# Query and key projected by channel, rotary on whole tiles, score operands stacked by SBUF-to-SBUF transfers, and the two tap chains interleaved

## The chip, the cores and the metric

The kernel runs on one core of one Trainium2 chip. The metric is device time in microseconds of one execution. Three runs of the kernel before gave a median of 925.05 us (922.57 to 925.73).

## The reference

Two layers of a decoder trunk over 512 tokens of width 1024, in float32. Each layer normalises the residual, projects it into nine blocks of 256 columns, feeds four token mixers with them, and projects the four outputs back onto the residual. Then come a routed mixture of 16 experts and a gated per-layer input. The change touches the differential attention and, in a detail, the 31-tap convolution:

```python
u = n @ w_in[i]                       # 1024 -> 9 x 256
a_val, a_gate, pool_in, q, k, v, gb, gc, sv = split(u)
# conformer: glu = a_val * sigmoid(a_gate); y = causal depthwise conv, 31 taps; layernorm; silu
# differential attention: 4 heads, 2 components each, 32 channels per component
rot = concat([-x[..., 16:], x[..., :16]])          # apply_rope, on q and on k
x   = x * cos + rot * sin
sc  = einsum("bqhcd,bkhcd->bhcqk", qb, k) * 32 ** -0.5
a   = softmax(where(mask, sc, -inf))
a   = a[:, :, 0] - lam * a[:, :, 1]
o   = einsum("bhqk,bkhe->bqhe", a, v)              # rmsnorm follows, then the output projection
```

## The kernel before

Every float32 operand of a large product is split into a high part that the matrix engine takes exactly and a low part that holds the rest. A product is then three matmuls: high by high, low by high, high by low (`mm3`). ScalarE makes the high part (a cast), VectorE the low part (a subtraction). This holds for weights too: `w.get` hands out one half of a weight load of 1 MB, split by a ScalarE cast (`wh`) and a VectorE subtraction (`wl`).

`project` forms the nine blocks. Most are projected by channel in `cm_unit`: the weight is the stationary operand and all 512 tokens stream past it, so that the output tile has channels on the partitions. Query and key are projected by token instead: the normalised tokens `nhi`, `nlo` are stationary and 512 weight columns stream past, into four tiles `o` of 128 tokens by 512 channels. The rotary embedding (`rotate`) works on half a token tile at a time with four VectorE operations on 128x128 or 128x256 elements.

`attend` needs query and key with channels on the partitions. For each of the 16 head components the score product is one matmul over 96 rows: three blocks of 32 rows that hold high, low, high of the query (`QT`) against high, high, low of the key (`KT`). Before the change `stack` and `stack_lo` write the three blocks side by side into the tile `qks` (two ScalarE operations and one VectorE subtraction for each token tile and side), and `qkt` turns them with TensorE transposes, four at a time, which ScalarE copies into `QT` and `KT`.

The order of the instructions is written by hand. The attention loop runs over 18 steps `n`; the list `TICK` gives the order of the parts of a step, and `ROT`, `STK`, `STL` say in which step which piece of rotary and stacking is done. The output projection (`wo_mm`) is the filler for TensorE: `filler(n, k)` issues k halves of six matmuls each, and `FILL1`, `FILL2` hold k for each step. VectorE's filler are the convolution's taps: 31 for each of two channel tiles, each one operation on 128x512 elements that adds to the accumulator `acc`. They wait in a queue from which `tick` takes as many as its budget allows, first all of channel tile 0, then all of tile 1. Weights come by transfers that SyncE issues in program order from one queue; where an instruction of that queue waits, all behind it wait.

Pools of SBUF are opened and closed as a stack on two sides. `KT` stands in the pool `kp`, which is opened where `ntp`, the pool of `nhi` and `nlo`, was closed.

Of the kernel before, what the change touches and what calls it, by code (L numbers as in the profile page):

```python
# [11 lines left out]
F32 = mybir.dt.float32  # L12
F32R = mybir.dt.float32r
# [26 lines left out]
K_ID, K_RC, K_IO, K_VT, K_DE, K_IW, K_MK, K_TRI, K_COS, K_SIN = 0, 128, 160, 288, 304, 320, 322, 450, 578, 834  # L40
NCON, NCON2, NCON3 = 322, 256, 512
# [6 lines left out]
FILL2 = [4, 0, 1, 0, 0, 1, 0, 4, 1, 0, 0, 1, 0, 0, 0, 1, 2, 1, 2, 1, 2, 2, 4, 2, 2, 2, 0, 0, 0]  # L48
# [4 lines left out]
TICK = "qkt max add av out exp f1 stl turn stk due lo rot score hi f2 comb".split()  # L53
TAPS = [1.8, 2.4, 2.4, 4.8, 1.8, 1.2, 5.4, 0, 0, 0.6, 3.6, 0, 0, 1.2, 3.4, 0, 1.0, 3.4]
ROT = {0: [(2, 0)], 2: [(2, 1)], 3: [(3, 1)], 4: [(3, 0)]}
STK = {0: [(1, 1)], 2: [(2, 0)], 3: [(2, 1)], 5: [(3, 0)], 7: [(3, 1)]}
STL = {1: [(1, 1)], 3: [(2, 0)], 5: [(2, 1)], 6: [(3, 0)], 8: [(3, 1)]}
# [110 lines left out]
class _Kernel:  # L168
# [91 lines left out]
    def run(self):  # L260
# [163 lines left out]
    def cm_unit(self, between=None, cost=0.0):  # L424
        o = [self.mm([128, S]) for _ in range(2)]
        for hf in range(2):
            self.cm_half(o, self.w.get(between=between if hf == 0 else None), hf)
            self.ticks.tick(BUDGET - cost if hf == 0 else BUDGET)
        return o

    def project(self):
# [165 lines left out]
        rope = vp.tile([128, 2, NT, 2, 32], F32, name="rope")  # L597
        nc.sync.dma_start(rope, self.A["con"][:, K_COS:K_COS + NCON3].rearrange("p (c t a d) -> p c t a d", c=2, t=NT, a=2))
        qr = self.qr = [vp.tile([128, 16, 32], F32, name=f"qr{i}") for i in range(NT)]
# [5 lines left out]
        def qk(i, half, k0):  # L605
            ts = slice(i * 128, (i + 1) * 128)
            hi, lo = (t.rearrange("p (c n) -> p c n", c=2) for t in half)
            for c in range(2):
                k = k0 + c
                self.mm3(o[i], self.nhi[:, k, ts], self.nlo[:, k, ts], hi[:, c], lo[:, c], k == 0, k == 7)  # L610

        half = w.get(between=ev_v)
        o = [self.mm([128, 512]) for _ in range(NT)]
        for hf in range(2):
            if hf:
                half = w.get()
            for i in range(NT):
                qk(i, half, 2 * hf)
            tk.tick(BUDGET)
        hv = [w.get(1), w.get(1)]  # L620
        for i in range(NT):
            for hf in range(2):
                qk(i, hv[hf], 4 + 2 * hf)
        w.make_hi(w.cur + 2)

        def rotate(i, b):

            bs = slice(8 * b, 8 * b + 8)
            x4 = qr[i][:, bs] if i else o[0].rearrange("p (a d) -> p a d", d=32)[:, bs]
            rt, rs = (vp.tile([128, 8, 32], F32, name=nm) for nm in ("rt", "rs"))  # L630
            cos, sin = rope[:, 0, i, b, None, :], rope[:, 1, i, b, None, :]
            V.tensor_mul(rs[:, :, 0:16], x4[:, :, 16:32], sin[:, :, 0:16].to_broadcast([128, 8, 16]))
            V.tensor_mul(rs[:, :, 16:32], x4[:, :, 0:16], sin[:, :, 16:32].to_broadcast([128, 8, 16]))
            V.tensor_mul(rt, x4, cos.to_broadcast([128, 8, 32]))
            V.tensor_add(qr[i][:, bs], rs, rt)

        self.rotate = rotate
        for b in range(2):
            rotate(0, b)
        for i in range(1, NT):  # L640
            SC.copy(qr[i].rearrange("p a d -> p (a d)"), o[i])
        w.make_lo()
        self.ntp.close_()
        self.banks(3, 1)

# [47 lines left out]
    def attend(self):  # L693
        V, T, SC, w, tk, sm, l = self.V, self.T, self.SC, self.w, self.ticks, self.sm, self.l
        mhi, mlo, h = self.mhi, self.mlo, self.h
        kp = self.pool("kp", side=self.side[0])
        KT = kp.tile([96, 8, S], F32R, name="KT")
        xp = self.xp
        a2 = self.pool("a2", side=self.side[1])
        QT = {}  # L700
        stk = {}


        qks = xp.tile([128, 2, 8, 3, 32], F32, name="qks", bufs=1)

        def stack(i, p):
            s_ = stk[i, p] = qks[:, p]
            SC.copy(s_[:, :, 0, :].bitcast(F32R), self.qr[i][:, 8 * p:8 * p + 8])
            SC.copy(s_[:, :, 2 - p, :], s_[:, :, 0, :])

        def stack_lo(i, p):
            s_ = stk[i, p]
            V.tensor_sub(s_[:, :, 1 + p, :].bitcast(F32R), self.qr[i][:, 8 * p:8 * p + 8], s_[:, :, 0, :])

        def qkt(i, p, b):
            s_ = stk[i, p]
            if p == 0 and b == 0:
                QT[i] = kp.tile([96, 8, 128], F32R, name="QT", bufs=2)
            pt = self.tr([128, 4, 128])
            for c in range(4):  # L720
                T.transpose(pt[:96, c], s_[:, 4 * b + c].rearrange("p a d -> p (a d)"), self.ident)
# [855 lines left out]
```

## Time and profile before

| | |
|---|---|
| median of three runs | 925.05 us |
| the profiled execution's own time | 925.41 us |
| span of its instructions | 923.6 us |
| mean granted TensorE clock | 0.973 of full speed |
| TensorE busy | 858.0 us, 93% |
| VectorE busy | 715.4 us, 77% |
| ScalarE busy | 519.1 us, 56% |

The profile is of one execution. Busy shares are averages over stages with different limits. What the change is worth is read from the stage that it touches, in each of the two layers: the end of the projections and the attention loop (in the first layer from about 99 to 200 us).

### The profile page before, as it was taken

The numbers are of one execution on the slowest core, as the hardware profiler recorded it, in microseconds if no ns is written. First come the engines' busy times: TensorE is split into PE (matmuls) and PEld (weight loads), VectorE is DVE, ScalarE is ACT, GpSimd is POOL, SyncE is SP. The second block draws the span as 40 slices with busy tenths as digits, with TensorE's granted clock in tenths as the row PEclk, the third lists the DMA queues.
The fourth block names the chain that finished last, engine by engine and source line by source line (L and its number), as shares of the span: only waits on it lengthen the run. The fifth ranks groups of instructions, "written<-read, shape, count | busy, mean of one in ns | idle before, by whom it ended". The sixth has DMA issues, their size and how long they took to land. (4 is left out here: it accounts for less than half of the span.)

```text
span 923.6 us, 12348 instructions
## 1 busy us (share of the span) xinstructions
PE 858.0 (93%) x4393; PEld 687.6 (74%) x4393; DVE 715.4 (77%) x1182; ACT 519.1 (56%) x945; POOL 151.2 (16%) x214
## 2 busy tenths in 40 slices
PE   7999988897999999979979999989979999998994
PEld 5888876685677777767878887767847777776783
DVE  4599989966788888746676998998478888885674
ACT  4322246853687878745433233487347778776453
POOL 2040001122222211101010300022131222111101
PEclk9999999998999999999999999989979999999998
DMA  9222230158799979563322223110958998882602
GB/s 354 106 92 96 98 114 1 46 193 309 270 347 363 370 271 340 227 234 146 114 92 92 92 103 112 49 46 24 373 216 307 359 370 324 317 321 91 260 24 91
DMA packets 35775, 179.02 MB, mean 194 GB/s; under 512 B 8064, under 2 KB 8320, under 8 KB 18944
## 3 DMA queue, kind: packets, MB, share of 16 engines
q1 hardware_dynamic: 23472, 148.49, 43.1%
q0 software_dynamic: 9792, 20.99, 6.2%
q10 hardware_dynamic: 2448, 8.73, 2.6%
q8 instruction: 35, 0.57, 0.2%
q14 instruction: 28, 0.23, 0.1%
HBM read 171.89 MB, written 23.07 MB: 211 GB/s over the span
## 5 line engine op out<-in xcount | busy, mean ns | idle before, releaser
L239 DVE TENSOR_TENSOR wl<-wr,wh 128x1024 fp32r<-128x1024 f32 x212 | 253.1, 1220 | 41.4 <-ACT wh L228 40.1
L228 ACT CAST wh<-wr 128x1024 fp32r<-128x1024 f32 x212 | 216.2, 1053 | 91.1 <-PE mm L256 60.9
L255 PE MATMUL mm<-wh,xTh 128*128 128x512 f32 x256 | 113.9, 445 | 1.0 <-ACT xTh L221 1.0
L483 DVE SCALAR_TENSOR_TENSOR acc<-glu,cwh,acc 128x512 f32<-128x512 f32 x120 | 100.5, 837 | 3.4
L257 PE MATMUL mm<-wh,xTl 128*128 128x512 f32 x256 | 101.2, 395 | 1.2 <-DVE xTl L222 1.2
L256 PE MATMUL mm<-wl,xTh 128*128 128x512 f32 x256 | 100.5, 392 | 0.0
L257 PE MATMUL mm<-nhi,wl 128*128 128x512 f32 (+1 forms) x224 | 77.3, 345 | 2.5 <-DVE wl L239 2.5
L255 PE MATMUL mm<-nhi,wh 128*128 128x512 f32 (+1 forms) x224 | 77.1, 344 | 0.0
L256 PE MATMUL mm<-nlo,wh 128*128 128x512 f32 (+1 forms) x224 | 77.0, 344 | 0.0
L255 PEld LDWEIGHTS mm<-wh,xTh 128*128 128x128 f32 x256 | 48.1, 188 | 16.9 <-issue 6.7
L1241 PE MATMUL mm<-wr,hT 128*128 128x512 f32 x128 | 60.2, 592 | 0.0
L1198 POOL DMA_INDIRECT xg<-xnd,ix x32 | 35.4, 1105 | 149.8 <-PE tr L251 136.8
L256 PEld LDWEIGHTS mm<-wl,xTh 128*128 128x128 f32 x256 | 48.2, 188 | 15.3 <-DVE wl L239 6.2
L257 PEld LDWEIGHTS mm<-wh,xTl 128*128 128x128 f32 x256 | 48.0, 188 | 12.9 <-DVE xTl L222 2.9
L255 PE MATMUL mm<-wh,mhi 128*128 128x512 f32 x128 | 54.0, 422 | 1.0 <-DVE h L750 1.0
L1203 POOL DMA_INDIRECT yd<-ys,ix x32 | 32.3, 1010 | 122.9 <-ACT ys L1243 107.3
L255 PE MATMUL mm<-wh,n3h 128*128 128x512 f32 x128 | 50.6, 395 | 0.0
L257 PE MATMUL mm<-wh,mlo 128*128 128x512 f32 x128 | 50.3, 393 | 0.0
L256 PE MATMUL mm<-wl,mhi 128*128 128x512 f32 x128 | 50.0, 391 | 0.0
L257 PE MATMUL mm<-wh,n3l 128*128 128x512 f32 x128 | 49.9, 390 | 0.0
L256 PE MATMUL mm<-wl,n3h 128*128 128x512 f32 x128 | 49.9, 390 | 0.0
L257 PEld LDWEIGHTS mm<-nhi,wl 128*128 128x128 f32 x224 | 42.4, 189 | 8.2 <-DVE wl L239 3.2
(236 smaller groups left out, 1861.6 us busy)
## 6 DMA issues: line engine op xcount, KB each, us to landing
wr<-wgu SPq DMA_DIRECT2D x62, 1024.0 KB, 9.1
wr<-wdn SPq DMA_DIRECT2D x30, 1024.0 KB, 10.8
wr<-win SPq DMA_DIRECT2D x13, 1024.0 KB, 6.2
wr<-wout SPq DMA_DIRECT2D x8, 1024.0 KB, 4.8
wr<-wpg SPq DMA_DIRECT2D x8, 1024.0 KB, 13.8
yt<-yd SPq DMA_DIRECT2D x12, 512.0 KB, 8.1
wr<-wqk SPq DMA_DIRECT2D x4, 1024.0 KB, 4.8
xnd<-xn ACTq DMA_DIRECT2D x8, 512.0 KB, 4.0
```

The costliest lines, as they stand in the source:

```text
L228: self.SC.copy(hi, src)
L239: self.V.tensor_sub(lo, src, h32)
L255: self.T.matmul(o, lh, rh, start=first, stop=False)
L256: self.T.matmul(o, lh, rl, start=False, stop=False)
L257: self.T.matmul(o, ll, rh, start=False, stop=last)
L483: V.scalar_tensor_tensor(acc[:, m], glu[:, m, k:k + S], self.cwh[:, m, k:k + 1], acc[:, m], op0=ALU.mult, op1=ALU.add)
L1198: return self.G.indirect_dma_start(out=dst, out_offset=None, in_=self.xnd[:, :], in_offset=bass.IndirectOffsetOnAxis(ap=col, axis=0), boun ...
L1203: return self.G.indirect_dma_start(out=self.yd[:, :], out_offset=bass.IndirectOffsetOnAxis(ap=col, axis=0), in_=src, in_offset=None, bound ...
L1241: self.T.matmul(o[nh], hT[:, c], wc[:, ns], start=(c == 0), stop=(c == 1))
```

## The change

The columns of query and key in the input weight are put in another order on the host, so that both can be projected with `cm_unit`. The two output tiles of such a unit hold the first and the second half of the 32 channels of all eight head components, 128 rows each. The rotary embedding then takes three VectorE operations on 128x512 elements for each of the two tiles, one ScalarE cast and one VectorE operation for the low part. The query's scale is applied in that cast. The rows of `QT` and `KT` are filled by transfers from SBUF to SBUF: each moves 128 rows of 512 floats, 256 KB, into 16 rows. There are six for the key and six for the query in a layer, all in SyncE's queue. `QT` now holds all 512 queries.

```diff
-            for u in (1, 0, 2, 7, 8, 6, 5):
+            for u in (1, 0, 2, 7, 8, 6, 5, 4, 3):
                 w.add(A["win"][l, u])
-            for kh in range(2):
-                w.add(A["wqk"][l, kh])
...
-            for m in range(2):
-                for k in range(31):
+            for k in range(31):
+                for m in range(2):
                     tk.queue.append((0.6, tap(m, k)))
...
+        def rotary(p, o):
+
+            hi, lo = parts[p][:, 0], parts[p][:, 1]
+            for m in range(2):
+                t = rp.tile([128, S], F32, name="rt", bufs=1)
+                V.tensor_mul(lo[:, m], o[m], rope[:, 0])
+                V.tensor_mul(t, o[1 - m], rope[:, 1])
+                V.tensor_tensor(lo[:, m], lo[:, m], t, op=ALU.add if m else ALU.subtract)
+                hr = hi[:, m].bitcast(F32R)
+                if p:
+                    SC.copy(hr, lo[:, m])
+                else:
+                    SC.activation(hr, lo[:, m], AF.Copy, scale=QSCALE)
+            for m in range(2):
+                lr = lo[:, m].bitcast(F32R)
+                if p:
+                    V.tensor_sub(lr, lo[:, m], hi[:, m])
+                else:
+                    V.scalar_tensor_tensor(lr, lo[:, m], QSCALE, hi[:, m], op0=ALU.mult, op1=ALU.subtract)
+
+        def stack(p):
+
+            st = (self.QT, self.KT)[p].bitcast(F32)
+            for a, part in sorted(enumerate(((0, 1, 0), (0, 0, 1))[p]), key=lambda x: x[1]):
+                for m in range(2):
+                    r = 32 * a + 16 * m
+                    nc.sync.dma_start(st[r:r + 16], parts[p][:, part, m])
+
+        o_k = self.cm_unit(ev_v)
+        o_q = self.cm_unit(lambda: rotary(1, o_k), 3.6, BUDGET)
+        w.make(w.cur + 2)
         self.ntp.close_()
+        self.kp = self.pool("kp", side=self.side[0])
+        self.KT = self.kp.tile([96, 8, S], F32R, name="KT")
+        self.QT = self.kp.tile([96, 8, S], F32R, name="QT")
+        stack(1)
         self.banks(3, 1)
+
+        def q_in():
+            rotary(0, o_q)
+            stack(0)
+            rp.close_()
...
-        for p in range(2):
-            stack(0, p)
-            stack_lo(0, p)
         wo_get(0, 0)
-        for p in range(2):
-            for b in range(2):
-                qkt(0, p, b)
-        filler(0, 2)
-        for p in range(2):
-            self.rotate(1, p)
+        filler(0, 1)
+        self.q_in()
+        a2 = self.pool("a2", side=self.side[1])
+        filler(0, PRE1)
         wo_get(0, 1)
-        stack(1, 0)
-        stack_lo(1, 0)
-        filler(0, 1)
```

`PRE1` is 5, the first entry of `FILL2` goes from 4 to 2, and the steps `qkt`, `rot`, `stk` and `stl` leave the list `TICK`.

The first place is TensorE's order at the end of the first layer's projections. Before, the last projection matmul is followed by 16 transposes (`tr<-con,qks`), three halves of the output projection, four more transposes and the first score matmul (`mm<-KT,QT`):

```order
L257 MATMUL mm<-wh,nlo 128x512
L721 MATMUL tr<-con,qks 96x128 x16
L255 MATMUL mm<-wh,mhi 128x512
...
L257 MATMUL mm<-wh,mlo 128x512
L721 MATMUL tr<-con,qks 96x128 x4
L762 MATMUL mm<-KT,QT 128x256
```

Of the change, with the semaphores that end each instruction's wait (a DMAHW semaphore counts a transfer of SyncE's or ScalarE's queue):

```order
L256 MATMUL mm<-nhi,wl 128x512
L254 MATMUL mm<-wh,mhi 128x512 [waits Activation_49]
L255 MATMUL mm<-wl,mhi 128x512 [waits DVE_49]
...
L254 MATMUL mm<-wh,mhi 128x512 [waits DVE_49]
...
L256 MATMUL mm<-wh,mlo 128x512
L738 MATMUL mm<-KT,QT 128x256 [waits DMAHW4_49,DMAHW3_49,DMAHW5_49,DMAHW2_49,DMAHW7_49,DMAHW1_49,DMAHW0_49]
```

The transposes are gone, 36 matmuls (six halves) stand between the projections and the first score matmul instead of 18, and that matmul now waits for transfers. The 13th of the 36 (the row in the middle that waits for DVE) takes a PSUM bank that the query's rotary reads last in its fifth operation.

The second place is SyncE's queue in the same stretch. Before, nothing stands between the last loads of the output weight and those of the experts:

```order
L114 DMA wr<-wqk 128x2048 x2
L114 DMA wr<-wout 128x2048 x2
L598 DMA rope<-con 128x512
L114 DMA wr<-wout 128x2048 x2
L114 DMA wr<-wgu 128x2048 x4
L114 DMA wr<-wdn 128x2048
```

Of the change, with waits (the row that stands for the third to sixth transfer of each group is left out where it reads alike but for the semaphore):

```order
L597 DMA rope<-con 128x1024 [waits DMAHW4_49,DVE_49,Pool_49]
L113 DMA wr<-wout 128x2048 [waits DMAHW1_49,DVE_49]
L630 DMA KT<-qk_971 16x8x512 [waits PE_49,Activation_49]
L630 DMA KT<-qk_971 16x8x512 [waits DMAHW5_49,DVE_49]
L113 DMA wr<-wgu 128x2048 [waits DMAHW6_49,DVE_49]
L630 DMA QT<-qk_970 16x8x512 [waits DMAHW7_49,Activation_49]
L630 DMA QT<-qk_970 16x8x512 [waits DMAHW4_49,DVE_49]
L113 DMA wr<-wgu 128x2048 [waits DMAHW5_49,DVE_49]
```

Six transfers for the key, one expert load of 1 MB and six transfers for the query stand in one queue. The first of the key waits for TensorE: `KT` lies where `nhi` and `nlo` lay, and the count that it waits for is that of the last projection matmul, of the query.

## Rows read from the trace of the kernel before

**Rows 1.** The page's first part: busy us, share of span, instructions.

```profile
PE 858.0 (93%) x4393; PEld 687.6 (74%) x4393; DVE 715.4 (77%) x1182; ACT 519.1 (56%) x945; POOL 151.2 (16%) x214
```

**Rows 2.** Windows, first layer: length, busy of PE, PEld, DVE, ACT, POOL, clock, DMA, GB/s.

```profile
99.10:120.90 21.80, 21.80 (x98) 17.85 (x96) 19.96 (x30) 5.43 (x9) 0.00 (x0) 1.00 0.29 99
120.90:129.50 8.60, 6.57 (x39) 5.32 (x39) 6.45 (x14) 6.65 (x13) 0.00 (x0) 1.00 0.43 170
129.50:157.00 27.50, 25.21 (x142) 19.73 (x140) 26.25 (x72) 14.03 (x45) 2.11 (x6) 1.00 0.11 39
157.00:184.00 27.00, 22.87 (x140) 18.52 (x140) 24.77 (x63) 24.00 (x69) 5.50 (x8) 0.94 0.11 40
```

**Rows 3.** Timeline of TensorE: start us, us, instruction, idle time before it and releaser.

```profile
119.76 0.39 PE L256 MATMUL mm<-wl,nhi 128*128 128x512 f32 x1
...
120.67 0.39 PE L257 MATMUL mm<-wh,nlo 128*128 128x512 f32 x1
122.64 1.93 PE L721 MATMUL tr<-con,qks 128*96 128x128 f32 x16 [1.59 <-DVE qks L713]
124.33 0.48 PE L255 MATMUL mm<-wh,mhi 128*128 128x512 f32 x1
...
129.52 0.36 PE L762 MATMUL mm<-KT,QT 96*128 96x256 f32 x1
```

**Rows 4.** Groups by line, whole span: count, busy us, mean ns, idle before.

```profile
L721 PE MATMUL tr<-con,qks 128*96 128x128 f32 x128 | 19.9, 289 | 6.1 <-DVE qks L713 4.1 <-ACT at L806 2.0
...
L222 DVE TENSOR_TENSOR nlo<-tr,nhi 128x512 fp32r<-128x512 f32 x16 | 10.3, 684 | 10.8 <-ACT nhi L221 10.8
...
L221 ACT CAST nhi<-tr 128x512 fp32r<-128x512 f32 x16 | 8.9, 588 | 17.4 <-PE tr L251 17.3
...
L713 DVE TENSOR_TENSOR qks<-qr,qks 128x256 fp32r<-128x256 f32 x16 | 6.7, 418 | 5.4 <-ACT qks L708 5.4
```

**Rows 5.** Timeline of VectorE, first layer: taps (L483, L480), a rotary block (L632), a maximum.

```profile
97.65 0.75 DVE L483 SCALAR_TENSOR_TENSOR acc<-glu,cwh,acc 128x512 f32<-128x512 f32 x1
98.31 0.54 DVE L480 TENSOR_SCALAR acc<-glu,cwh,par 128x512 f32<-128x512 f32 x1
...
99.90 4.68 DVE L483 SCALAR_TENSOR_TENSOR acc<-glu,cwh,acc 128x512 f32<-128x512 f32 x6
104.50 1.22 DVE L239 TENSOR_TENSOR wl<-wr,wh 128x1024 fp32r<-128x1024 f32 x1
...
132.54 0.28 DVE L632 TENSOR_TENSOR rs<-qr,rope 128x128 f32<-128x128 f32 x1
...
133.75 0.48 DVE L770 TENSOR_REDUCE mx<-mm 128x1 f32<-128x128 f32 x2
```

**Rows 6.** Timeline of SyncE's queue, two stretches: start us, us of issuing.

```profile
541.71 0.33 SPq L598 DMA_DIRECT2D rope<-con  x1
...
852.08 5.55 SPq L1363 DMA_DIRECT2D yt<-yd  x10
```

**Rows 7.** Transfers of 542 to 545 us: busy tenths in 40 slices; issue, KB, us to landing.

```profile
DMA  0000000036490694489998632100000000000000
...
rope<-con SPq DMA_DIRECT2D x1, 256.0 KB, 2.7
```

**Rows 8.** Transfers of 915 to 917.5 us, the same view.

```profile
DMA  0000000009999499996999969799400000000000
...
out<-xn SPq DMA_DIRECT2D x1, 512.0 KB, 2.6
```

**Rows 9.** Windows at the first layer's routing, columns as in rows 2.

```profile
216.00:220.00 4.00, 4.00 (x36) 3.78 (x34) 1.88 (x2) 2.27 (x5) 0.74 (x2) 1.00 1.01 428
...
224.00:228.00 4.00, 1.03 (x14) 0.68 (x15) 3.39 (x12) 0.00 (x0) 0.00 (x0) 0.50 0.72 288
228.00:232.00 4.00, 4.00 (x11) 1.36 (x9) 3.86 (x10) 0.00 (x0) 2.64 (x2) 0.50 0.00 0
```

More of the change, by code (lines that the diff above doesn't have):

```diff
@@ L51 @@
 HI = {5: 1, 6: 2, 9: 3, 10: 4}
-TICK = "qkt max add av out exp f1 stl turn stk due lo rot score hi f2 comb".split()
+TICK = "max add av out exp f1 turn due lo score hi f2 comb".split()
 TAPS = [1.8, 2.4, 2.4, 4.8, 1.8, 1.2, 5.4, 0, 0, 0.6, 3.6, 0, 0, 1.2, 3.4, 0, 1.0, 3.4]
-ROT = {0: [(2, 0)], 2: [(2, 1)], 3: [(3, 1)], 4: [(3, 0)]}
-STK = {0: [(1, 1)], 2: [(2, 0)], 3: [(2, 1)], 5: [(3, 0)], 7: [(3, 1)]}
-STL = {1: [(1, 1)], 3: [(2, 0)], 5: [(2, 1)], 6: [(3, 0)], 8: [(3, 1)]}
+PRE1 = 5
 OUTD = [1, 2, 3, 4]
@@ L422, in cm_first, with cm_unit @@
                                       start=ps == 0 and k == 0, stop=ps == 2 and k == 7)
-    def cm_unit(self, between=None, cost=0.0):
+    def cm_unit(self, between=None, *costs):
         o = [self.mm([128, S]) for _ in range(2)]
-        for hf in range(2):
+        for hf, cost in zip(range(2), costs + (0.0, 0.0)):
             self.cm_half(o, self.w.get(between=between if hf == 0 else None), hf)
-            self.ticks.tick(BUDGET - cost if hf == 0 else BUDGET)
+            self.ticks.tick(BUDGET - cost)
         return o
@@ L596, in project @@
         self.vt = [vp.tile([128, 256], F32, name=f"v{i}") for i in range(NT)]
-        rope = vp.tile([128, 2, NT, 2, 32], F32, name="rope")
-        nc.sync.dma_start(rope, self.A["con"][:, K_COS:K_COS + NCON3].rearrange("p (c t a d) -> p c t a d", c=2, t=NT, a=2))
-        qr = self.qr = [vp.tile([128, 16, 32], F32, name=f"qr{i}") for i in range(NT)]
+        rp = self.rp = self.pool("rp", side=Y)
+        rope = rp.tile([128, 2, S], F32, name="rope")
+        nc.sync.dma_start(rope, self.A["con"][:, K_COS:K_COS + NCON3].rearrange("p (c t) -> p c t", c=2))
+        parts = [rp.tile([128, 2, 2, S], F32, name=f"qk{p}") for p in range(2)]
         def ev_v():
@@ L603, in ev_v @@
                 SC.copy(self.vt[i], o_v[i])
[L605 to L635, printed above, removed]
@@ L695, in attend @@
         mhi, mlo, h = self.mhi, self.mlo, self.h
[L696 to L721, printed above, removed]
-            hs = slice(4 * b, 4 * b + 4)
-            SC.copy(QT[i][:, hs] if p == 0 else KT[:, hs, i * 128:(i + 1) * 128], pt[:96])
+        KT, QT, xp = self.KT, self.QT, self.xp
         CH = [[2, 3, 6, 7], [0, 1, 4, 5]]
@@ L761, in scores @@
                 keys = KT[:, 2 * hd + c, :k] if qi else KT[:, 2 * hd + c, None, :128].to_broadcast([96, 2, 128])
-                T.matmul(pt[:, :k], QT[qi][:, 2 * hd + c], keys, start=True, stop=False)
+                T.matmul(pt[:, :k], QT[:, 2 * hd + c, qs_], keys, start=True, stop=False)
                 T.matmul(pt[:, qs_], self.identb, self.maskb, start=False, stop=True)
@@ L942, in turns @@
                 turn(n - 2)
-        def each(table, f):
-            def g(n):
-                for a in table.get(n, ()):
-                    f(*a)
-            return g
         steps = {
             "av": lambda n: n >= 3 and av(n - 3),
-            "qkt": lambda n: n < NS - 4 and qkt(n // 4 + 1, n % 4 // 2, n % 2),
             "out": o_start,
@@ L960, in attend @@
             "comb": lambda n: 1 <= n <= NS and comb(n - 1),
-            "rot": each(ROT, self.rotate),
-            "stk": each(STK, stack),
-            "stl": each(STL, stack_lo),
             "lo": lambda n: w.make_lo(),
@@ L1488, in _constants @@
     ang = pos[:, None] * inv[None, :]
-    ang = np.concatenate([ang, ang], -1)
-    cs, sn = np.cos(ang).astype(f), np.sin(ang).astype(f)
-    sn[:, :16] = -sn[:, :16]
-    both = np.array([32.0 ** -0.5, 1.0], f)[:, None]
-    for at, t in ((K_COS, cs), (K_SIN, sn)):
-        t = t.reshape(NT, 128, 1, 32) * both
-        c[:, at:at + 256] = t.transpose(1, 0, 2, 3).reshape(128, 256)
+    for at, t in ((K_COS, np.cos(ang)), (K_SIN, np.sin(ang))):
+        c[:, at:at + S] = np.repeat(t.astype(f).T, 8, 0)
     for m in range(2):
```

22 lines of the change are left out of this document (9 added, 13 removed).

## The prediction

> **What bounds the kernel now.** The page's first part comes first [rows 1]: TensorE is busy for 93% of the span, VectorE for 77%. Such averages don't say what the touched stretch is worth, so the windows of the first layer come next [rows 2]. During the projection of query and key (99.1 to 120.9) TensorE is busy all the time; nothing gained on VectorE shows there. From 120.9 to the first score matmul at 129.5 TensorE is idle for 2.0 us of 8.6. In the attention loop the reader is to see a change of limit: from 129.5 to 157 VectorE is busy for 26.25 of 27.5 us, from 157 to 184 for 24.77 of 27, while TensorE has 2.3 and 4.1 us idle. So the loop is held by VectorE, with TensorE (and, late, ScalarE at 24.0 of 27) close behind.
>
> The timeline of TensorE gives the order at the seam [rows 3]. Two 512-column matmuls start 0.23 us apart ((120.67 - 119.76) / 4), so the projections end at T = 120.9. TensorE waits for the stacked query, transposes 16 times (122.64 to 124.33, 1.69 us, or 0.42 for four), does 18 filler matmuls and reaches the first score at T + 8.6. A half of the filler is six matmuls, 1.37 us.
>
> **What the change removes.** TensorE: 64 transposes in a layer (128 in the trace [rows 4]), 16 groups of four: 1.7 us before the first score, and 12 x 0.42 = 5.0 us in the loop. VectorE in the loop: four rotary blocks of 1.21 us (132.54 to 133.75) [rows 5], 4.8 us, and five subtractions of 0.42 us [rows 4], 2.1 us. The taps: six that each need the one before take 4.60 us to the next instruction (99.90 to 104.50), while an instruction that follows a tap of the other channel tile starts 0.66 us after it (97.65 to 98.31) [rows 5]; so a dependent tap costs (4.60 - 0.66) / 5 = 0.79, an independent one 0.66, and the 12 taps of the loop save 1.5 us. That the 50 others also shorten is worth nothing, since TensorE covers them [rows 2]. Sum on VectorE: 8.4 us for each layer. TensorE has room for it (6.4 us idle and 5.0 us of transposes), but VectorE itself already idles for 2.2 us in the second window, where steps wait for other engines; so I take 6.5 us, with 4 and 8.4 as bounds. The ScalarE work that goes lies beside this.
>
> Neutral: the two projections. Before 96 matmuls of 512 columns, after twice 48; the same four weight loads. The key's rotary lies under the query's projection (10.9 us): six VectorE operations of about 0.68 and two of the low part [rows 4] are 5.5 us, in place of two rotary blocks (2.4). VectorE was busy for 19.96 of 21.8 us there, the taps give back about 2; I let it run 1 us late. If that cover were gone, nothing would happen to the key, whose transfers wait for T in any case.
>
> **What the change adds on the path.** The first score matmul waits for all twelve transfers, since each writes all heads and tokens of its 16 rows. The key's first waits for T (its target lies over the normalised tokens). Behind it stand five more of the key, an expert load of 1 MB and six of the query, in one queue. The query's own chain, about 1 us after T: three operations for the first tile and its cast (2.1 + 0.6) put the first high part at T + 4, the last low part at T + 7. The queue comes to it no earlier than that, so its VectorE work is hidden under the key's transfers; without that cover it would cost those 7 us.
>
> The time of the transfers, from the nearest rows. From issue to first data 0.9 us (541.71 to slice 8 of 75 ns, 542.60); 0.45 from the last data (slice 25, 543.95) to landing at 2.7 [rows 6, 7]. The 1 MB load at 428 GB/s [rows 9] takes 2.45. For one transfer of 256 KB, d: no row shows one from SBUF to SBUF, or into 16 rows. Lower end: 512 KB out of SBUF took 20 slices of 62.5 ns [rows 8], 1.25 us with all 16 engines, so d = 0.63. Upper end: if the 16 target rows take only what four of 16 engines bring, d = 2.5. The nearest row is the rotary table's load, the same 256 KB in the same queue: 18 slices, d = 1.35 [rows 7]. I take that. Issuing does not bind: 13 x 0.56 = 7.2 us at the slowest rate seen [rows 6].
>
> First score: T + 0.9 + 12 x 1.35 + 2.45 + 0.45 = T + 20.0. To compare with before: at T + 8.6 three halves of the filler were done, now six; the equal point is T + 8.6 + 3 x 1.37 = T + 12.7. So 7.3 us are lost. TensorE itself has work to T + 10.1 (12 matmuls 2.7 us, then a wait to T + 4.6 for the bank that the rotary still reads, then 24 matmuls 5.5), and so idles for about 10 us. Longer idle lowers its clock: in 224 to 228, with 1.03 us of work in 4, the granted clock is 0.50 (1.2 GHz), and 228 to 232, full of work, still runs at 0.50 [rows 9]. Four microseconds at half speed lose 2; I add 2.
>
> Sum for a layer: +7.3 - 6.5 + 2.0 = +2.8. Both layers have the same code: +5.6. On the profiled execution's own 925.4 (1.8 over its span; 0.4 above the median of 925.05) that is **931 us**.
>
> **The rivals.** *Transfers at the engines' full rate* (d = 0.63): first score at T + 0.9 + 7.6 + 2.9 = T + 11.4, 1.3 before the equal point, no long idle and no clock loss: -7.8 for a layer, **910 us**. For it: SBUF gave 410 GB/s in rows 8, and the table's 1.35 holds the delay of external memory, which these transfers don't have. Against: there the other side was not 16 rows. It decides from where 12 d falls under 8.9 + 4.5, d about 1.1.
>
> *A quarter of the rate* (d = 2.5): first score at T + 33.8, 21.1 lost, +16.6 for a layer, **959 us**. For it: all 16 engines write into 16 neighbouring rows at a time, so that only few lanes into SBUF work; nothing in the rows speaks against it, since every transfer there has 128 rows or engines of their own. The Trainium skill, page "SBUF — State Buffer", section "Door 1: The DMA port swizzle", states such a rule: 16 partitions reach 4 of the 16 ports, and 104 GB/s was measured there; by it 256 KB take 2.5 us and the sum is that of this rival. No row of this trace shows a transfer into so few partitions. Between it and the forecast lies all that happens if engines get out of step and write several blocks of rows at once.
>
> *The change gives nothing in the loop*: if ScalarE or the chain of the softmax steps holds it after all, 6.5 falls to 4 and the forecast rises to 936; this lies inside the range.
>
> **How the numbers follow.** Forecast (d from about 1.1 to 1.9): 0.38, with 922 to 944 as its own range. Full rate: 0.35, 905 to 921. Quarter rate: 0.27, 945 to 962. For the range I leave out the ends: **908 to 959**. A measurement can tell about 0.3%, 2.8 us. Faster by more than that: 0.35 and 0.02 of the forecast's case, 0.37. Within it: 0.11 of the forecast's case. Slower: 0.25 of it and 0.27, 0.52.
>
> **What would show it.** Right: the key's first transfer issued at the end of the query's projection; the first score matmul about 20 us after that, released by a transfer; 18 slices' worth of data for each 256 KB; TensorE idle for 10 us before it and its clock at half behind it; taps 0.66 us apart; the loop from the first score to the output norm 6 to 7 us shorter. Wrong: a first score before T + 13 (full rate; the loop's gain then stands alone), or after T + 28 (quarter rate); or a loop that keeps its length, which would say that VectorE did not hold it.

## The result: 960 us, 3.8% slower, and the profile after

The changed kernel takes 960.09 us (median of four runs, 959.38 to 962.25) against 925.39 before; the ratio is 1.0377, with an interval from 1.0337 to 1.0416. The profiled execution took 960.32 us, its span is 958.2 us and its mean granted clock 0.945.

TensorE's busy share falls (it is [rows 1] that answers to this row of the page):

```profile
PE 850.0 (89%) x4265; PEld 680.1 (71%) x4265; DVE 703.6 (73%) x1134; ACT 493.0 (51%) x883; POOL 155.1 (16%) x214
```

TensorE has 8 us less work and the span is 34.6 us longer, so it waits some 43 us more. The timeline of TensorE at the seam, where [rows 3] showed the kernel before (start us, us, instruction, idle time before it and what ended it), says where:

```profile
120.81 0.39 PE L256 MATMUL mm<-nhi,wl 128*128 128x512 f32 x1
...
125.03 0.50 PE L254 MATMUL mm<-wh,mhi 128*128 128x512 f32 x1 [1.10 <-DVE rt L610]
...
130.37 0.39 PE L256 MATMUL mm<-wh,mlo 128*128 128x512 f32 x1
152.79 0.55 PE L738 MATMUL mm<-KT,QT 96*128 96x256 f32 x1 [22.03 <-DMA QT<-qk]
```

The projections end at T = 120.81 + 0.23 = 121.04. The filler is done at T + 9.6, and then TensorE waits 22.03 us for a transfer into `QT`. The first score comes at T + 31.75. Before, with T reckoned alike (120.67 + 0.23 = 120.90, [rows 3]), it came at T + 8.62. The second layer has the same, with its first score at T + 31.5:

```profile
620.65 0.55 PE L738 MATMUL mm<-KT,QT 96*128 96x256 f32 x1 [23.23 <-DMA QT<-qk]
```

SyncE's queue in the first layer's stretch (issuing alone):

```profile
121.28 3.89 SPq L630 DMA_DIRECT2D KT<-qk  x6
125.26 0.55 SPq L113 DMA_DIRECT2D wr<-wgu  x1
125.91 9.24 SPq L630 DMA_DIRECT2D QT<-qk  x6
```

All thirteen transfers are issued by 135.2; it is the data that takes until 151. The view of transfers gives GB/s in 40 slices of 0.4 us, from 121 to 137 and from 137 to 153:

```profile
GB/s 41 0 0 0 200 236 246 102 108 128 169 97 97 133 92 169 118 118 97 108 133 154 97 123 108 102 159 133 102 102 123 118 148 149 210 82 102 225 532 389
```

```profile
GB/s 369 389 348 348 128 97 123 108 113 154 123 108 118 108 143 128 118 113 97 128 164 108 97 123 108 159 128 108 102 118 128 154 128 210 92 82 246 328 328 532
```

The reader is to see two plateaus at a little over 120 GB/s (the key's six transfers, the query's six) with the load of 1 MB at 350 to 530 between them. The mean of the 8th to the 34th slice of the first row is 121.7 GB/s, so 256 KB take 2.15 us (2.17 by the packets themselves, the figure in the expectations below). Only the first three slices of the key's stretch, after a pause, run at 200 to 246. The sum up to the first score, read to a slice of 0.4 us: 1.8 us until the key's data runs, 12.0 for its six, 3.8 for the load, 12.6 for the query's six, 1.6 until the matmul starts.

What follows the wait, in windows (length, busy of PE, PEld, DVE, ACT, POOL, clock, DMA, GB/s), from T to the loop's last product with the values at 221.87:

```profile
121.04:130.60 9.56, 8.46 (x37) 6.49 (x35) 8.31 (x12) 2.20 (x3) 0.00 (x0) 1.00 0.91 115
130.60:152.79 22.19, 0.16 (x2) 0.03 (x1) 3.34 (x5) 0.00 (x0) 0.00 (x0) 0.56 1.07 169
152.79:180.79 28.00, 25.96 (x126) 20.01 (x126) 21.51 (x59) 13.14 (x47) 4.31 (x9) 0.92 0.04 16
180.79:206.79 26.00, 23.66 (x129) 19.33 (x130) 23.73 (x58) 20.23 (x56) 5.06 (x9) 0.80 0.12 41
206.79:221.87 15.08, 15.08 (x100) 13.10 (x100) 8.53 (x21) 8.29 (x21) 2.32 (x6) 1.00 0.63 244
```

The loop, from the first score on, lasts 69.08 us. In the kernel before the same stretch lasts from 129.52 to 204.45; the sum row of its windows:

```profile
sum 74.93, PE 68.49 PEld 55.92 DVE 64.48 ACT 51.15 POOL 11.92; mean PE 22.83 PEld 18.64 DVE 21.49 ACT 17.05 POOL 3.97
```

So the loop is 5.85 us shorter (6.7 in the second layer), and VectorE works 53.8 us in it instead of 64.5. First layer: 31.75 - 8.62 = 23.1 lost, 5.85 gained, 17.3 in all. Second layer: 22.9 lost, 6.7 gained, 16.2. Together they are 33.5 of the 34.6 us by which the spans differ; the other 1.1 us lie outside (0.1 ahead of T, -0.8 between the layers, 1.8 behind the second loop).

A second thing in the loop is much weaker in the kernel before, where [rows 2] have a clock of 0.94 at the lowest. In the middle of the loop TensorE works 2.42 of 4 us (178 to 182), and behind that its granted clock falls to 0.5, which is 1.2 GHz:

```profile
178.00:182.00 4.00, 2.42 (x15) 1.56 (x13) 3.93 (x11) 3.42 (x10) 0.36 (x1) 1.00 0.00 0
182.00:186.00 4.00, 3.19 (x19) 2.70 (x19) 3.89 (x12) 3.62 (x12) 1.13 (x4) 0.81 0.79 262
186.00:195.00 9.00, 8.69 (x34) 6.76 (x32) 8.75 (x22) 7.92 (x22) 1.94 (x1) 0.52 0.01 2
```

And the taps: four in turn, and the rotary that follows them.

```profile
111.60 2.74 DVE L480 SCALAR_TENSOR_TENSOR acc<-glu,cwh,acc 128x512 f32<-128x512 f32 x4
114.25 0.69 DVE L609 TENSOR_TENSOR qk<-mm,rope 128x512 f32<-128x512 f32 x1
```

They stand (114.25 - 111.60) / 4 = 0.66 us apart, where [rows 5] had 0.79 in a chain.

### The profile page after: what moved, and what is told of

The parts are those of the page before. It is cut to its first block, busy times and chain, and to the rows that moved or that the text cites. A ratio compares the mean times of both kernels' runs of the same rounds, so it can differ in the third digit from the quotient of the medians.

```text
span 958.2 us, 12015 instructions
## 1 busy us (share of the span) xinstructions
PE 850.0 (89%) x4265; PEld 680.1 (71%) x4265; DVE 703.6 (73%) x1134; ACT 493.0 (51%) x883; POOL 155.1 (16%) x214
## 5 line engine op out<-in xcount | busy, mean ns | idle before, releaser
L256 PE MATMUL mm<-nhi,wl 128*128 128x512 f32 (+1 forms) x288 | 102.1, 355 | 2.5 <-DVE wl L238 2.5
L254 PE MATMUL mm<-nhi,wh 128*128 128x512 f32 (+1 forms) x288 | 102.1, 354 | 0.0
L255 PE MATMUL mm<-nlo,wh 128*128 128x512 f32 (+1 forms) x288 | 101.9, 354 | 0.0
L480 DVE SCALAR_TENSOR_TENSOR acc<-glu,cwh,acc 128x512 f32<-128x512 f32 x120 | 90.5, 818 | 0.1
L760 ACT ACTIVATE e<-mm,mx 128x128 f32<-128x128 f32 (+3 forms) x64 | 33.1, 522 | 87.0 <-DVE mx L746 86.9
L738 PE MATMUL mm<-KT,QT 96*128 96x256 f32 (+2 forms) x64 | 26.2, 453 | 46.3 <-DMA QT<-qk 45.3
L256 PEld LDWEIGHTS mm<-nhi,wl 128*128 128x128 f32 x288 | 54.4, 189 | 10.7 <-DVE wl L238 3.1
L255 PEld LDWEIGHTS mm<-nlo,wh 128*128 128x128 f32 x288 | 54.5, 189 | 7.4
L254 PEld LDWEIGHTS mm<-nhi,wh 128*128 128x128 f32 x288 | 54.5, 189 | 7.3
L746 DVE TENSOR_REDUCE mx<-mm 128x1 f32<-128x128 f32 (+3 forms) x64 | 28.4, 483 | 42.0 <-PE mm L739 42.0
## 6 DMA issues: line engine op xcount, KB each, us to landing
wr<-wpg SPq DMA_DIRECT2D x8, 1024.0 KB, 12.5
```

The source lines that it names most:

```text
L254: self.T.matmul(o, lh, rh, start=first, stop=False)
L255: self.T.matmul(o, lh, rl, start=False, stop=False)
L256: self.T.matmul(o, ll, rh, start=False, stop=last)
L480: V.scalar_tensor_tensor(acc[:, m], glu[:, m, k:k + S], self.cwh[:, m, k:k + 1], acc[:, m], op0=ALU.mult, op1=ALU.add)
L738: T.matmul(pt[:, :k], QT[:, 2 * hd + c, qs_], keys, start=True, stop=False)
L746: V.tensor_reduce(mx[:, c:c + 1], st[n][c][:, :k], axis=AX, op=ALU.max, negate=True)
```

## The experiments

Theory P: 16 neighbouring target rows share a few ways into SBUF, and that sets the 2.15 us. Theory S, its rival: a transfer from SBUF to SBUF costs that wherever it goes. All runs stand in one table. "Wait" is the first score's distance from T, "loop" the length from there to the last product with the values and "clock" the granted clock in it, each for layer 1 and 2. These three are of the one profiled execution; the ratio is to runs of the kernel before on the same occasion.

| kernel | median us | ratio to before, interval | wait us | loop us | clock |
|---|---|---|---|---|---|
| before | 925.4 | 1 | 8.62, 8.62 | 74.9, 75.7 | 0.98, 0.95 |
| the change | 960.09 | 1.038 (1.034 to 1.042) | 31.8, 31.5 | 69.1, 68.9 | 0.89, 0.90 |
| e1 every 2nd row | 940.16 | 1.016 (1.013 to 1.020) | 20.0, 19.9 | 70.2, 70.5 | 0.86, 0.86 |
| e2 every 6th row | 938.62 | 1.015 (1.011 to 1.018) | 19.2, 19.0 | 68.6, 70.0 | 0.90, 0.88 |
| e3 two queues | 954.07, one run | | 26.8, 27.2 | 72.1, 68.8 | 0.84, 0.90 |
| e4 before, taps in turn | 924.72 | 0.9986 (0.9965 to 1.0008) | 8.62, 8.62 | 73.8, 73.7 | 1.00, 1.00 |
| e5 e2, load behind | 932.78 | 1.008 (1.006 to 1.010) | 16.4, 16.2 | 70.4, 69.5 | 0.86, 0.91 |
| e6 e5, token halves | 918.68 | 0.991 (0.989 to 0.993) | 10.6, 10.6 | 68.4, 69.1 | 0.90, 0.88 |
| e7 e6, neighbouring rows | 932.76 | 1.007 (1.005 to 1.009) | 15.0, 15.0 | 69.1, 74.3 | 0.89, 0.83 |
| e8 e6, scores again | 917.29 | 0.992 (0.989 to 0.995) | 10.6, 10.6 | 70.3, 70.5 | 0.90, 0.90 |
| e9 e6, filler spread | 913.01 | 0.9875 (0.985 to 0.990) | 10.5, 10.6 | 66.4, 65.6 | 0.95, 0.95 |
| e10 e6, taps in a chain | 930.78 | 1.007 (1.005 to 1.009) | 14.3, 12.5 | 69.0, 72.3 | 0.90, 0.86 |
| e11 full rows | 927.21 | 1.0007 (0.999 to 1.002) | 14.7, 15.1 | 69.2, 68.9 | 0.89, 0.90 |
| e12 e9, query from ScalarE | 919.33 | 0.993 (0.991 to 0.995) | 11.4, 11.5 | 68.8, 69.3 | 0.95, 0.95 |

**e1 and e2: the same transfers into other rows.** Query and key only have to agree on the order of the 96 rows, so the 16 rows of a transfer may lie anywhere.

```diff
-                    r = 32 * a + 16 * m
-                    nc.sync.dma_start(st[r:r + 16], parts[p][:, part, m])
+                    nc.sync.dma_start(st[32 * a + m:32 * a + 32:2], parts[p][:, part, m])   # e1
+                    nc.sync.dma_start(st[2 * a + m:96:6], parts[p][:, part, m])             # e2
```

> Each of the twelve transfers still moves 256 KB from 128 rows into 16 rows, but the 16 rows are every second one of a block of 32 instead of 16 neighbours. Theory P, that the neighbouring target rows share a few ways into SBUF: twice as many ways, so one transfer takes about half of the 2.17 us measured after the change, 1.1 us; the first score matmul comes 12.9 us earlier, at about 19 us behind the end of the projections, and each layer loses by about 13 to 15 us less: 930 to 936 us. Rival S, that a transfer of 256 KB from SBUF to SBUF costs 2.17 us wherever its 16 rows lie (both of its ends load the same memory, or 16 rows as such are slow): no change, 960 us.

> The same again with every sixth of all 96 rows as the 16 targets. Theory P: at most two rows share a way and both halves of the partitions are written, so a transfer takes between 0.63 us (the rate at which 512 KB left SBUF before) and 1.1 us; first score at about 12 to 19 us behind the end of the projections, 908 to 930 us. Rival S: 2.17 us a transfer and 960 us.

GB/s in slices of 0.4 us, e1 from 121 us and e2 from 122:

```profile
GB/s 41 0 0 10 200 225 400 266 220 195 215 195 220 189 215 195 230 251 225 205 225 297 246 287 430 430 369 451 297 338 210 225 200 210 200 256 220 230 205 205
```

```profile
GB/s 246 41 0 0 0 174 215 389 317 225 215 225 266 230 210 205 215 236 282 225 220 323 230 266 430 430 410 430 287 358 256 236 205 215 215 246 282 230 205 205
```

The plateau of 121 is now at 200 to 250 GB/s, with nothing changed but row numbers: the first score comes 11.7 us earlier in e1 and 12.5 in e2. Theory S falls. The time of e1 lies 4 us above its range and that of e2 9 us above: every sixth row is hardly better than every second (1.13 against about 1.2 us for 256 KB by the packets). The map of partitions to ports in the Trainium skill, page "SBUF — State Buffer", section "Door 1: The DMA port swizzle", would give that: by it 16 neighbours lie in 4 ports with four rows each, and in both spreads the fullest port has two. The measured rates agree nearly: 121 / 4 = 30 GB/s for a port in the change and about 29 for the fullest one in e2 (two rows of 16 KB in 1.13 us). Both lie above the page's 27.2. The runs show that the row numbers set the rate; that ports do it, with each of 16 engines writing a row of its own and all in step, is a reading of these numbers, since the trace names neither ports nor engines.

**e3: two queues.** `m = 1` is issued by ScalarE.

```diff
+                    q = nc.scalar if m else nc.sync
-                    nc.sync.dma_start(st[r:r + 16], parts[p][:, part, m])
+                    q.dma_start(st[r:r + 16], parts[p][:, part, m])
```

> Every second transfer is issued by ScalarE instead of SyncE, so that two transfers into different blocks of 16 rows are under way at a time; rows as in the changed kernel. Theory P in its simple form: two blocks have twice the ways in, so the twelve transfers together take 13 us instead of 26 and the time falls to 930 to 936 us. Rival Q, that the engines behind the two queues are the same 16 and one blocked write holds up what comes behind it in either: 26 us as before, 958 to 962 us. (The Trainium skill, page 'DMA: Bandwidth & Descriptors', section 'Issuing engines are not separate DMA queues', says that transfers from several issuers end up on the same engines and gain only the time of issuing; by it rival Q holds.)

GB/s in slices of 0.8 us from 121:

```profile
GB/s 0 0 138 220 115 133 115 120 133 131 154 126 120 128 118 149 179 72 333 394 440 404 366 212 215 215 205 215 215 207 223 256 307 358 471 21 0 0 0 0
```

Neither theory is right alone. The key's stretch stays at 115 to 154; there the packets come mostly from one queue for some 2 us and then from the other. The query's stays at 205 to 223, and there both queues' packets alternate all the time. So here two queues nearly doubled the rate only where transfers into different blocks were under way together. The sentence of the Trainium skill in the expectation is borne out by the first stretch and not by the second. The time of the single run, 954 us, lies between the two expectations.

**e4: the taps alone, on the kernel before.**

```diff
-            for m in range(2):
-                for k in range(31):
+            for k in range(31):
+                for m in range(2):
                     tk.queue.append((0.6, tap(m, k)))
```

> The kernel before with one part of the change alone: the taps of the two channel tiles in turn. Theory V, that VectorE holds the attention loop: the 12 taps in the loop save 0.13 us each, 1.5 us for each layer, and what a budget counted in taps lets through stays the same, so 921 to 923 us. Rival C, that the loop is held by the chain of softmax steps and by TensorE: no change, within 0.3% of 925 us.

In the profiled executions the loop is 1.1 and 2.0 us shorter, which looks like theory V. But e4's loops ran at a clock of 1.00 and those of before at 0.98 and 0.95, and the longer difference goes with the lower clock. The median falls by 0.1 us only, and the interval reaches from -3.2 to +0.7. This is inconclusive between the theories.

**e5 to e7: what stands in the queue ahead of the first score.** In e5 (on e2) the expert load waits until the query's transfers are issued; in e6 each transfer is cut by tokens, and the tile `rt` is placed once instead of in each pass; e7 is e6 with the rows of the change.

```diff
-        w.limit = self.moe_start[l] + 3
+        w.limit = self.moe_start[l]                       # e5, e6, e7
         wo_get(0, 0)
         filler(0, 1)
         self.q_in()
+        w.limit = self.moe_start[l] + 3
...
+        rt = rp.tile([128, 2, S], F32, name="rt")[:, 0]   # e6, e7
...
-                t = rp.tile([128, S], F32, name="rt", bufs=1)
+                t = rt
...
-        def stack(p):
+        def stack(p, hs):                                 # e6, e7
+            ts = slice(hs * 256, hs * 256 + 256)
...
-                    nc.sync.dma_start(st[r:r + 16], parts[p][:, part, m])
+                    nc.sync.dma_start(st[2 * a + m:96:6, :, ts], parts[p][:, part, m, ts])   # e6
+                    nc.sync.dma_start(st[32 * a + 16 * m:32 * a + 16 * m + 16, :, ts], parts[p][:, part, m, ts])   # e7
...
-        stack(1)
+        stack(1, 0)                                       # e6, e7
...
-            stack(0)
+            for p, hs in ((0, 0), (0, 1), (1, 1)):
+                stack(p, hs)
```

> As every sixth row, and the expert load of 1 MB stands behind the query's transfers instead of between the key's and the query's. Theory O, that the first score waits for the sum of what stands in the queue ahead of it: it comes 3 us earlier (the load's packets took 130.4 to 133.4 us), so each layer gains 3 us and up to 1 us of clock: 930 to 933 us against 938.6. Rival W, that the experts then wait for the load that starts later, or that the query's low part is not there yet when the queue gets to it: 936 to 940 us.

> As the one before, and each transfer is cut in two by tokens: first the twelve for tokens 0 to 255, which the first eight steps of the loop need, then the twelve for tokens 256 to 511, while the loop runs (the operands of the first score are half as many bytes; the half tiles' buffers are placed so that no step overwrites what a transfer still reads). Theory O: twelve transfers of 128 KB at about 0.6 us each, first score about 10 to 11 us behind the end of the projections, before the equal point of 12.7 us, and the loop keeps its gain of about 6 us: 912 to 921 us, faster than the kernel before. Rival D, that the time goes with the number of packets and not their bytes (packets of 1 KB take as long as those of 2 KB): 13 us for twelve, first score at about 16 us, 930 to 933 us.

> The cut by tokens and the load behind it, but with the rows as the change has them (16 neighbours). Theory P: 1.09 us for each 128 KB, twelve take 13 us, first score at 15 to 16 us behind the end of the projections: 924 to 930 us, slower than the same with spread rows by some 10 us. If the row numbers did not matter any more once half of the bytes are off the path, both would be equal within 2 us.

The first score in e5, e6 and e7:

```profile
137.33 0.55 PE L737 MATMUL mm<-KT,QT 96*128 96x256 f32 x1 [6.66 <-DMA QT<-qk]
```

```profile
131.45 0.36 PE L740 MATMUL mm<-KT,QT 96*128 96x256 f32 x1 [0.81 <-issue]
```

```profile
136.60 0.55 PE L740 MATMUL mm<-KT,QT 96*128 96x256 f32 x1 [5.24 <-issue]
```

Theory O holds: the wait falls from 19.2 to 16.4 and to 10.6 us, and e6 is faster than the kernel before. With neighbouring rows the wait is 4.4 us longer and the time 14 us; the row numbers still matter on half the bytes. Part of the 14 is the second layer's loop of 74.3 us (clock 0.83), where the first exponential waits for a transfer that still reads its buffer:

```profile
593.40 0.37 ACT L762 ACTIVATE e<-mm,mx 128x128 f32<-128x128 f32 x1 [14.74 <-DMA QT<-qk]
```

It comes 6.1 us behind the first score of that layer (587.34); in e7's first layer it comes after 1.0 us and waits for no transfer. In the second layer of e6 it waits for one too, 3.95 us behind the first score (579.03):

```profile
582.98 0.37 ACT L762 ACTIVATE e<-mm,mx 128x128 f32<-128x128 f32 x1 [8.26 <-DMA KT<-qk]
```

So the placing of buffers that the expectation speaks of does its work in the first layer alone; the second has its sides of the memory exchanged. In e6 the twelve transfers are issued 0.65 us apart (3.90 us for six), 7.8 of the 10.6 us. TensorE's own filler ends at T + 9.6, so little of that wait is left to gain.

**e8 and e9: the clock in the loop.** In e6 the middle of the loop reads

```profile
158.50:174.20 15.70, 14.64 (x57) 11.56 (x58) 15.16 (x39) 12.95 (x38) 3.08 (x5) 0.57 0.20 68
```

that is, half clock, TensorE and VectorE both full. e8 adds work there (the score matmuls of steps 6 to 10 three times), e9 moves filler there.

```diff
-                T.matmul(pt[:, :k], QT[:, 2 * hd + c, qs_], keys, start=True, stop=False)
+                for r in range(3 if 6 <= n <= 10 else 1, 0, -1):                                # e8
+                    T.matmul(pt[:, :k], QT[:, 2 * hd + c, qs_], keys, start=True, stop=r > 1)
```
```diff
-FILL1 = [0, 1, 1, 1, 1, 1, 0, 5, 1, 1, 1, 1, ...
+FILL1 = [0, 1, 1, 1, 1, 1, 1, 1, 1, 1, 1, 1, ...                                               # e9
-FILL2 = [2, 0, 1, 0, 0, 1, 0, 4, 1, 0, 0, 1, ...
+FILL2 = [1, 0, 0, 0, 0, 0, 0, 0, 0, 0, 0, 1, ...
```

> As the token halves, and in steps 6 to 10 of the loop each of the two score matmuls is issued three times into the same bank, each time with the same values, so that TensorE has about 0.5 to 0.9 us more work in each step. Theory K, that TensorE's thinner work behind the removed transposes lets its clock fall to 0.50 in the loop (in the token halves about 160.8 to 174 us in the first layer) and that this costs time: the clock stays at 1.00 there, the stretch is not TensorE's any more, and the time falls by 2 to 8 us against the token halves. Rival V, that VectorE (1.9 of 2 us busy there) holds these steps at either clock: the time stays within 2 us of the token halves or rises.

> As the token halves, and the ten halves of the filler that the first eight steps of the loop take are given out as one for each of the steps 0 to 9, so that steps 8 and 9 have one too. No work is added. Theory K: no stretch at half the clock between 156 and 174 us, 2 to 6 us for both layers less than the token halves. Rival V: within 2 us of the token halves, or the half clock only moves to an earlier step.

Windows of e8, then of e9 (the last row lies inside the first):

```profile
158.00:162.00 4.00, 1.89 (x13) 1.32 (x14) 3.86 (x11) 3.08 (x11) 0.00 (x0) 1.00 0.47 156
162.00:176.00 14.00, 14.00 (x53) 11.46 (x54) 11.70 (x29) 10.01 (x27) 3.08 (x5) 0.51 0.08 32
```

```profile
132.34:158.50 26.16, 23.31 (x119) 17.86 (x120) 24.03 (x65) 13.58 (x48) 4.32 (x9) 0.93 0.41 136
158.50:174.20 15.70, 13.65 (x72) 10.57 (x71) 15.27 (x40) 12.44 (x35) 3.07 (x5) 0.89 0.21 68
174.20:198.73 24.53, 24.51 (x166) 21.09 (x166) 16.79 (x37) 15.56 (x38) 4.31 (x9) 1.00 0.38 151
...
140.00:144.00 4.00, 3.80 (x14) 2.60 (x13) 3.37 (x9) 0.72 (x5) 0.00 (x0) 0.58 0.96 395
```

e8 did not test theory K: the added matmuls came ahead of the gap (1.89 of 4 us) and behind it, not into it, and the clock still fell to 0.51 for 14 us. Its time is within 1.4 us of e6, as rival V has it. e9 has 0.89 in that stretch and a loop of 66.4 and 65.6 us, 2.0 and 3.5 less than e6; against the kernel before it is 0.9875 where e6 is 0.991. A part of the half clock has only moved, as rival V allows: from 140 to 144 e9 has 0.58, where e6 has 1.00. Over the whole loop the clock is 0.95 in e9, and 0.90 and 0.88 in e6.

e9 changes both the clock and the filler's place, so by itself it does not tell them apart. Loops with the same code do. The change, e1, e2, e3 and e11 have the same order of instructions in the loop and 353 matmuls each (windows of e2 and e3 from the first score to the last product, then of the kernel before and e4):

```profile
141.73:210.34 68.61, 64.47 (x353) 52.34 (x354) 53.66 (x135) 41.69 (x121) 11.72 (x23) 0.90 0.20 77
148.06:220.18 72.12, 68.57 (x353) 55.42 (x354) 53.83 (x135) 41.64 (x121) 11.69 (x23) 0.84 0.19 72
...
581.07:656.72 75.65, 69.85 (x418) 57.09 (x416) 64.61 (x163) 51.24 (x143) 11.89 (x23) 0.95 0.22 82
580.58:654.27 73.69, 67.44 (x418) 54.66 (x416) 63.73 (x163) 51.05 (x143) 11.93 (x23) 1.00 0.22 84
```

Their ten loops last 68.6 to 69.2 us at 0.89 to 0.90, 70.0 to 70.5 at 0.86 to 0.88, and 72.1 at 0.84. In the longer ones the same matmuls keep TensorE busy for longer (64.47 against 68.57 us). With the time at half clock reckoned as (1 - clock) x length / 0.5, a straight line through the ten gives, as an estimate, 0.3 us of loop for each us at half clock and 64 to 65 us at full clock. e9 has about 7 us at half clock where e6 has 14 and 17; at 0.3 this is 2 to 3 us, about what e9's loops gain. This supports theory K, and by this estimate the clock accounts for most of e9's gain; that the clock alone was changed holds for no run. At 913.01 us e9 is the fastest version here.

**e10: the taps in one chain, on e6** (the edit of e4 undone).

> As the token halves, and the taps in one chain after the other, as before the change. Theory V, that VectorE holds the loop once the wait is gone: the 16 taps in the first four steps cost 0.13 us more each, 2 us for each layer, 3 to 5 us more than the token halves. Rival C, that taps give nothing there either, as in the kernel before with interleaved taps (924.72 against 924.86 us): within 2 us.

VectorE before the rotary of the key in e10, the rotary in e6, and e10's wait for the query's:

```profile
111.43 4.68 DVE L480 SCALAR_TENSOR_TENSOR acc<-glu,cwh,acc 128x512 f32<-128x512 f32 x6
116.03 0.68 DVE L610 TENSOR_TENSOR qk<-mm,rope 128x512 f32<-128x512 f32 x1
```

```profile
114.11 0.68 DVE L610 TENSOR_TENSOR qk<-mm,rope 128x512 f32<-128x512 f32 x1
```

```profile
126.79 0.79 PE L254 MATMUL mm<-wh,mhi 128*128 128x512 f32 x1 [2.83 <-DVE rt L611]
```

The median is 12 us above that of e6, more than theory V expected and in another place. The taps of the projection stage run longer, the key's rotary starts at 116.03 instead of 114.11, the query's two us later than in e6, its transfers too, and the first score comes 3.7 and 1.9 us later. The loop adds 0.6 and 3.2, in the second layer at a clock of 0.86 against 0.88. These 9.4 us are of the profiled execution, the fastest of e10's six (926.1 us); what the others add no trace shows.

**e11: what is left without the rows.** The stacking is left out: the transfers go into 128 rows.

```diff
-        self.KT = self.kp.tile([96, 8, S], F32R, name="KT")
+        self.KT = self.kp.tile([128, 6, S], F32R, name="KT")      # QT alike
...
-            for a, part in sorted(enumerate(((0, 1, 0), (0, 0, 1))[p]), key=lambda x: x[1]):
-                for m in range(2):
-                    r = 32 * a + 16 * m
-                    nc.sync.dma_start(st[r:r + 16], parts[p][:, part, m])
+            for t, (part, m) in enumerate(((0, 0), (0, 1), (0, 0), (0, 1), (1, 0), (1, 1))):
+                nc.sync.dma_start(st[:, t], parts[p][:, part, m])
```

> The changed kernel with the stacking left out: each of the twelve transfers moves its 256 KB from 128 rows into 128 rows (one of six columns of a tile), in the same queue, with the load of 1 MB between them, and the scores take 96 of these rows, so they are not those of the reference. It asks what is left of a transfer's time when the target rows are no limit. If the spread 16 rows (1.13 to 1.17 us) were still held by the rows written: 0.63 to 1.0 us each, first score at 12 to 17 us behind the end of the projections, 918 to 932 us. If packets of 2 KB or the reading side hold it: 1.1 to 1.2 us again, first score at 19 to 20 us and 936 to 941 us.

GB/s in slices of 0.4 us from 121, and the first score:

```profile
GB/s 440 307 154 31 0 118 410 405 410 405 400 410 400 374 415 353 61 143 143 287 389 307 307 307 241 210 317 343 405 405 405 405 400 410 440 420 481 425 410 471
```

```profile
136.59 0.58 PE L737 MATMUL mm<-KT,QT 96*128 96x256 f32 x1 [5.04 <-DMA QT<-qk]
```

The key's six run at 400 to 415 GB/s, 0.65 us each. So reading SBUF is not what holds the others, nor are packets of 2 KB; what differs is the target rows, in the spread layouts too. The wait is still 14.7 us, since the load's megabyte stands in the middle and the query's data starts only at about 130.9. And the kernel is then no faster than the one before (ratio 0.999 to 1.002).

**e12: the query's first six from ScalarE's queue, on e9.** `stack` takes the queue as its third argument, and one half of the filler moves into the loop.

```diff
-FILL2 = [1, 0, ...
+FILL2 = [2, 0, ...
-PRE1 = 5
+PRE1 = 4
...
-            for p, hs in ((0, 0), (0, 1), (1, 1)):
-                stack(p, hs)
+            stack(0, 0, nc.scalar)
+            for p in range(2):
+                stack(p, 1)
```

> As the spread filler, and the query's first six transfers are issued by ScalarE while SyncE issues the key's, with one half of the filler moved from ahead of the first score to the first step. Theory I, that the first score now waits for the issuing of twelve transfers one after the other (0.65 us each on SyncE): first score at 8.5 to 9.5 us instead of 10.6, and up to 1.5 us less for each layer: 910 to 913 us. Rival A, that the waits now standing in ScalarE's queue hold up the weight cast behind them and so the next weights: 913 to 918 us.

ScalarE issues, and casts the next weight behind that; VectorE waits for the cast, TensorE for a transfer:

```profile
126.31 4.41 ACTq L631 DMA_DIRECT2D QT<-qk  x6
130.76 1.04 ACT L227 CAST wh<-wr 128x1024 fp32r<-128x1024 f32 x1 [3.88 <-DMA QT<-qk]
```

```profile
131.84 1.23 DVE L238 TENSOR_TENSOR wl<-wr,wh 128x1024 fp32r<-128x1024 f32 x1 [4.23 <-ACT wh L227]
```

```profile
132.99 0.36 PE L741 MATMUL mm<-KT,QT 96*128 96x256 f32 x1 [3.08 <-DMA QT<-qk]
```

The cast is at 130.76 where e9 has it at 127.05, and VectorE waits 4.23 us for it: the delay that rival A speaks of is there. The first score itself waits for a query transfer, at 11.4 instead of 10.5, since ScalarE can issue the six only behind the query's casts (from 126.31; SyncE had done with the key's at 125.7). What theory I expected did not come. The loop lasts 68.8 and 69.3 us at e9's clock, 2.4 and 3.7 more; the half of the filler that moved into it (1.4 us) and VectorE's work pushed there by the late cast are both in that, and no run tells them apart. The time (919.33) is above rival A's range.

## Why the prediction was wrong

**What failed: the value taken for d.** The forecast was 931 us with a range of 908 to 959; the measured 960.09 lies just above it. The forecast took 1.35 us for a transfer, from the nearest row; in steady succession it is 2.17, and the twelve together took 24.6 us instead of 16.2. That nearest row was near in bytes and queue, but it filled 128 rows. The rival with a quarter of the rate named what was to come (few ways into 16 neighbouring rows); that the row numbers decide, e1, e2 and e11 show. It was weighed at 0.27, because no row of before had a transfer into so few rows. The sentence of the Trainium skill beside that rival (four ports, 104 GB/s) was the only evidence that bore on it; the measured 121 GB/s is 16% above that figure.

**The rival's 959 is in part luck.** Its twelve transfers were 5.4 us too long (30.0 against 24.6), its load, start and end 3.4 too short, and its loop 2.75 too good, all for the first layer.

**The sum, term by term, for the first layer.** Forecast +2.8, measured +17.3. The first score came at T + 31.75, not T + 20.0: the twelve transfers took 24.6 us instead of 16.2 (+8.4), the load 3.8 instead of 2.45 (+1.35), the start 1.8 instead of 0.9, and the end 1.6 instead of 0.45 (+2.05). Before, it came at 8.62, as forecast (8.6). That is 11.75 of the 14.5 us.

**The second term that was mis-sized: the clock.** The other 2.75 us are in the loop. The forecast took 6.5 us off it for VectorE's work and credited 4.1 us for three halves of filler done ahead of the first score, 10.6 together; for the clock it added 2.0, from four microseconds at half speed. That is 8.6 net, and the loop shows 5.85 with all of this in it (6.7 in the second layer). At a clock of 0.89 it has about 15 us at half speed, not 4, and at the 0.3 us estimated above they cost about 4.5. At full clock the same estimate gives 64 to 65 us, 9 to 10 less than the 73.8 of e4, which ran at full clock; so the 10.6 were nearly right. This division rests on the line through ten loops and not on an experiment of its own. That VectorE holds the changed loop the runs do not show: it works 53.8 of 69.1 us there.

**What was right.** The key's first transfer goes out at 121.28, at the end of the query's projection, and its rotary lies under that. The query's chain ends at 127.1, T + 6.05 (T + 7 forecast), under the key's transfers. The bank that the rotary still reads comes free at T + 4.0 (4.6). TensorE's clock is at half after the wait (0.58 from 152.79 to 158). The taps are 0.66 us apart. VectorE's work in the loop falls by 64.5 - 53.8 = 10.7 us; 2.7 of that are the four taps that now stand ahead of the first score, 1.3 are two additions to the residual that moved there with the filler, and 6.7 remain against 8.4.

**What had been called worth nothing and is not.** "That the 50 others also shorten is worth nothing, since TensorE covers them": in the kernel before no gain clear of noise was seen (e4). In the new order the rotary stands behind those taps, and where the first score is close behind the rotary, as in e6, they cost 1.9 to 3.7 us of wait (e10).

**What the full-rate rival left out.** e11 has its d, and ends at 927 and not 910: its first score comes at T + 14.7 and not T + 11.4, since the load, the start and the end were too cheap, and its loop is 5.75 us shorter, with the clock at 0.89, where the rival had no loss of clock.

## What to carry to other kernels

Before work moves from an engine to transfers, ask into which rows each writes, not only how many bytes; where an order of rows is free, spread them, and cut a transfer so that the first consumer waits only for what it reads (here 960 became 919 us so, with the load put behind as well and no engine doing less). A row that is near in bytes and queue is no price for a transfer whose rows lie otherwise. Where work is taken from TensorE, look at the granted clock through the whole stretch behind, and try to spread what filler is left.

## What the runs showed of the hardware beyond that

Two queues did not double the rate into 16-row blocks while whole transfers took turns (115 to 154 GB/s), and nearly did when their packets alternated (205 to 223); what decides between the two stays open. Every sixth of 96 rows gave hardly more than every second of 32 (1.13 and about 1.2 us). The key's first transfer in the change, after a pause, ran at about twice the rate of those behind it (200 to 246 against 121 GB/s); why, stays open. Loops of the same 353 matmuls lasted from 68.6 us (granted clock 0.90) to 72.1 us (0.84).
